# Gate and up projections of a feed-forward layer by seven half-size products

## The chip, the cores and the metric

The kernel runs on one core of a Trainium2 chip. The metric is device time in microseconds (us), the median of the runs. TensorE is called PE, its weight loads PEld, VectorE DVE, ScalarE ACT, GpSimd POOL, SyncE SP; a queue that issues DMAs has a q behind its name (SPq).

## The reference, cut to what matters

Two layers (D = 1024, hidden size 2816) work on x (512 tokens) and, beside it, on a context xc (256 tokens). Each layer has a first feed-forward half step, four mixers of 256 columns each, and a second feed-forward half step; modulation columns come from c. All is float32. The context's second half is computed in the first layer alone.

```
def swiglu(h, wg, wu, wd):
    return (jax.nn.silu(h @ wg) * (h @ wu)) @ wd
...
x = x + 0.5 * mx[2] * swiglu(pre_norm(x, norm1_g[i], mx[0], mx[1]), ffn1_wg[i], ffn1_wu[i], ffn1_wd[i])
xc = xc + 0.5 * mc[2] * swiglu(pre_norm(xc, norm1_g[i], mc[0], mc[1]), ffn1_wg[i], ffn1_wu[i], ffn1_wd[i])
...
x = x + 0.5 * mx[8] * swiglu(pre_norm(x, norm3_g[i], mx[6], mx[7]), ffn2_wg[i], ffn2_wu[i], ffn2_wd[i])
```

## The kernel before

All activations lie transposed: model columns on the partitions, tokens along the free dimension. "A" is x with 512 tokens, with halves A0 and A1 of 256, and "C" is the context with 256 (UNITS, line 28). To keep float32's accuracy on PE, each operand is split into a high and a low part of type float32r (`split`, line 262: the cast on ACT, the low part on DVE by a subtraction), and one product is three matmuls (`mm3`, line 284): high by high, high by low, low by high.

An FFN (`ffn`, line 291) runs four times: the first half step of layer 0 on A and C, the second of layer 0 on A and C, the first of layer 1 on A and C, the second of layer 1 on A alone. It has 22 blocks f of 128 hidden columns, in four groups (GROUPS, line 21: 6, 6, 5, 5). For a block, two weights of 128 x 1024 (gate and up) are loaded by SP and split (`weight`, line 273, three buffers of each kind), and PE runs 8 contraction steps of `mm3` for gate and up, on C (256 columns) and on A (512 columns): 96 matmuls. ACT takes the silu of the gate from PSUM, DVE multiplies it by up (line 323), and the result `h` is split into `hh` and `hl`. After a group, the down projection runs for the 8 output tiles m: one weight of 128 x (128 times the group's blocks), `mm3` over the blocks into `dacc`, and DVE adds the gated result into X in SBUF (line 344). In the last group the down projection goes over its weights once for C, once for A0 and once for A1 (PASSES, line 27), each time loading and splitting them again, so that the norm of a finished part (`then`) can start while the next part is computed.

Beside that run the modulation columns: `ada` (line 145) is a generator; `fill` (line 195) takes steps of it in proportion to the blocks done. A step loads 128 x 1024 weights by a DMA that POOL issues (four buffers, AB, line 23) and makes one or two reductions over 1024 elements on DVE (line 160). The first modulation columns are made at the start by PE from 32 tiles of 256 KB (`ada_first`, line 130), in the buffers of the hidden rows.

The order of instructions in each engine's queue is not that of the text: the whole program is traced, each instruction with its place in the text as its priority, and a scheduler lays out the queues at build time along a timeline that it simulates (`schedule_with_timeline_sim`, line 1569). An instruction that is ready can be drawn ahead of an earlier one that is not. Buffers of one tag are reused in turn; an instruction waits for the release of its buffer.

PSUM has eight banks in three rings (BANKS, line 29: p 4, r 2, d 2). Between the FFNs lie the output projection of the mixers (`second_half`, line 1384) and the mixers (`mixers`, line 1454) with the projections `proj` (line 427); `perm` there reads A's tokens in another order, in runs of 16.

## Time and profile before

| | us |
|---|---|
| median of 3 runs | 3223.46 |
| lowest, highest | 3222.37, 3239.32 |
| the profiled execution's own time | 3218.36 |
| its span, first to last instruction | 3216.6 |
| PE busy in it | 3092.6 |
| DVE busy in it | 1670.6 |
| ACT busy in it | 1061.2 |
| POOL busy in it | 391.3 |
[...]

The profile is of one execution. Busy time of an engine is the union of its instructions. Matmuls overlap in the pipeline, and their ends are modelled, so the step from one start to the next is the better measure of their cost. A row `A<-B,C` names the tile that is written and the tiles that are read; L270 is line 270 of the kernel.

### The profile page before, as it was taken

Reading aid. Unit: us, or ns where it says so; the run is one execution under the profiler, and the core shown is the slowest. Engines: PE = TensorE matmul, PEld = TensorE weight load, DVE = VectorE, ACT = ScalarE, POOL = GpSimd, SP = SyncE. Lnnn points to the kernel's source line nnn. Section 1 sums busy time; section 2 is a strip of 40 time slices with the busy share of each in tenths; the row PEclk is TensorE's granted clock in tenths of the full one; section 3 lists DMA queues with packets and bytes.
Section 4 is the critical chain, followed back from the end, with each engine's and each line's share of the span. In section 5 each row is a group of like instructions: output and inputs, shape, how many; then the busy total and the mean of one; then the engine's idle time right before and its main releaser. Section 6 shows DMA issues by size and latency. Waiting matters only on the chain.

```text
span 3216.6 us, 48071 instructions
## 1 busy us (share of the span) xinstructions
PE 3092.6 (96%) x19394; PEld 2699.5 (84%) x19394; DVE 1670.6 (52%) x2964; ACT 1061.2 (33%) x1912; POOL 391.3 (12%) x646
## 2 busy tenths in 40 slices
PE   7999999998999999999999999999997899999998
PEld 4888888886788888888889988888885788788887
DVE  4994232736855449994236332323646745353334
ACT  3212112545444433121224212122455353342223
POOL 1110000410233011120002000000311332000001
PEclk9999999998999999999999999999998999899999
DMA  6662221514543335683124221212523523323333
GB/s 246 200 204 59 70 68 48 176 56 125 153 98 89 85 127 180 202 264 120 53 73 125 61 64 60 73 53 68 149 74 121 149 73 83 122 87 99 96 99 105
DMA packets 133485, 358.42 MB, mean 111 GB/s; under 512 B 17968, under 2 KB 31792, under 8 KB 132880
## 3 DMA queue, kind: packets, MB, share of 16 engines
q1 hardware_dynamic: 101200, 256.52, 26.0%
q0 software_dynamic: 32064, 98.85, 10.9%
q8 instruction: 152, 2.49, 0.3%
q14 instruction: 69, 0.57, 0.1%
HBM read 317.94 MB, written 39.65 MB: 111 GB/s over the span
## 4 chain that ended last, share of the span: by engine, by line
PE 55%; DVE 3%; DMA 1%; ACT 1%; issue 1%; POOL 0%; SPq 0%; POOLq 0%; DVEq 0%; ACTq 0%
PE dacc L286 4%; PE dacc L287 4%; PE dacc L288 4%; PE uA L288 4%; PE uA L286 4%; PE uA L287 4%; PE gA L287 4%; PE gA L286 4%; PE gA L288 4%; PE guC L288 3%; PE guC L286 3%; PE guC L287 3%; PE o L738 2%; PE pj L286 1%; PE pj L288 1%; PE pj L287 1%
## 5 line engine op out<-in xcount | busy, mean ns | idle before, releaser
L265 ACT CAST wh<-wr 128x1024 fp32r<-128x1024 f32 (+5 forms) x443 | 394.8, 893 | 1262.9 <-PE dacc L287 452.8
L270 DVE TENSOR_TENSOR wl<-wr,wh 128x1024 fp32r<-128x1024 f32 (+5 forms) x443 | 459.6, 1040 | 411.3 <-ACT wh L265 391.0
L286 PE MATMUL dacc<-hh,wh 128*128 128x256 f32 (+1 forms) x1392 | 451.3, 326 | 1.7 <-ACT wh L265 1.5
L288 PE MATMUL dacc<-hh,wl 128*128 128x256 f32 (+1 forms) x1392 | 450.7, 326 | 1.4 <-DVE wl L270 1.3
L287 PE MATMUL dacc<-hl,wh 128*128 128x256 f32 (+1 forms) x1392 | 452.1, 326 | 0.0
L286 PE MATMUL guC<-xnhC,wh 128*128 128x256 f32 x1056 | 298.8, 284 | 3.3 <-ACT xnhC L259 1.7
L288 PE MATMUL guC<-xnhC,wl 128*128 128x256 f32 x1056 | 299.4, 284 | 0.9 <-DVE wl L270 0.9
L287 PE MATMUL guC<-xnlC,wh 128*128 128x256 f32 x1056 | 299.0, 283 | 0.0
L160 DVE CUSTOM_DVE_ANT_0 adao<-adaw,silr,adab 128x1024 f32<-128x1024 f32 x224 | 287.1, 1282 | 11.8 <-DMA adaw<-ada_t 8.5
L286 PE MATMUL gA<-xnhA,wh 128*128 128x512 f32 (+1 forms) x752 | 284.2, 379 | 2.0 <-ACT xnhA L259 2.0
L286 PEld LDWEIGHTS dacc<-hh,wh 128*128 128x128 f32 x1392 | 261.4, 188 | 27.7 <-ACT wh L265 2.6
L287 PE MATMUL gA<-xnlA,wh 128*128 128x512 f32 (+1 forms) x752 | 282.9, 378 | 1.0 <-DVE xnlA L260 1.0
L288 PEld LDWEIGHTS dacc<-hh,wl 128*128 128x128 f32 x1392 | 261.2, 188 | 26.9 <-DVE wl L270 2.0
L288 PE MATMUL uA<-xnhA,wl 128*128 128x512 f32 (+1 forms) x752 | 283.0, 376 | 0.6 <-DVE wl L270 0.6
L286 PE MATMUL uA<-xnhA,wh 128*128 128x512 f32 (+1 forms) x752 | 283.1, 376 | 0.4 <-ACT wh L265 0.4
L287 PE MATMUL uA<-xnlA,wh 128*128 128x512 f32 (+1 forms) x752 | 283.1, 376 | 0.0
L288 PE MATMUL gA<-xnhA,wl 128*128 128x512 f32 (+1 forms) x752 | 282.8, 376 | 0.0
L287 PEld LDWEIGHTS dacc<-hl,wh 128*128 128x128 f32 x1392 | 261.4, 188 | 25.0
L344 DVE SCALAR_TENSOR_TENSOR xA<-dacc,modG,xA 128x512 f32<-128x512 f32 (+1 forms) x160 | 102.1, 641 | 253.5 <-PE dacc L288 253.2
L286 PEld LDWEIGHTS guC<-xnhC,wh 128*128 128x128 f32 x1056 | 202.3, 192 | 7.4 <-ACT wh L265 2.4
L287 PEld LDWEIGHTS guC<-xnlC,wh 128*128 128x128 f32 x1056 | 202.9, 192 | 2.7
L288 PEld LDWEIGHTS guC<-xnhC,wl 128*128 128x128 f32 x1056 | 203.0, 192 | 1.9 <-DVE wl L270 1.5
(352 smaller groups left out, 5737.7 us busy)
## 6 DMA issues: line engine op xcount, KB each, us to landing
wr<-wgu SPq DMA_DIRECT2D x176, 512.0 KB, 3.6
adaw<-ada_t POOLq DMA_DIRECT2D x128, 512.0 KB, 4.4
wr<-wd SPq DMA_DIRECT2D x120, 320.0 KB, 3.0
wr<-wd SPq DMA_DIRECT2D x64, 384.0 KB, 3.2
wr<-win SPq DMA_DIRECT2D x44, 512.0 KB, 3.7
adaw<-ada_w SPq DMA_DIRECT2D x32, 256.0 KB, 5.2
hl<-eh SPq DMA_DIRECT2D x32, 192.0 KB, 3.1
...
```

Of the source, the lines that this page charges most:

```text
L160: nc.vector.tensor_tensor_reduce(o, w, self.silr[:, v], 1.0, self.adab[:, l, m:m + 1], ALU.mult, ALU.add, self.mods[l][:, m, v:v + 1])
L265: nc.scalar.copy(hi, src)
L270: (nc.vector if leng == "V" else nc.gpsimd).tensor_tensor(lo, src, hi.bitcast(F32), op=ALU.subtract)
L286: nc.tensor.matmul(out, lhsT=wh, rhs=xh, start=start, stop=False)
L287: nc.tensor.matmul(out, lhsT=wh, rhs=xl, start=False, stop=False)
L288: nc.tensor.matmul(out, lhsT=wl, rhs=xh, start=False, stop=stop)
L344: nc.vector.scalar_tensor_tensor(out=x, in0=acc, scalar=gate[:, i, m, r:r + 1], in1=x, op0=ALU.mult, op1=ALU.add)
L738: nc.tensor.matmul(o[:, q0 + q], lhsT=p[:, q * 128:q * 128 + 128], rhs=v(kb), start=False, stop=kb == 3 and q == n // 128 - 1)
```

## The change

The three FFNs that work on A and C get a new function, `ffn2`; the last one, on A alone, keeps `ffn` without its context parts. Blocks 0 to 2 are computed plainly, the other 19 by Strassen's scheme (in Winograd's form) with seven products in place of eight. The 2 x 2 blocks of the weight are (gate, up) by the two halves of the contraction, those of the activation are the two halves of the contraction by two halves of the tokens: 256 of A and 128 of C each, 384 columns. So xn is now laid out as two tiles of 4 contraction steps x 2 halves x 384 tokens for each part. `sums7` makes the activation's sums once per FFN, on DVE and POOL (x21 is overwritten with a sum after the plain blocks); `chunk7` makes the weight's sums for each block on DVE, splits seven blocks of 128 x 512, and runs seven products of 4 x 3 matmuls, with additions between the PSUM banks' contents on DVE. It yields after each product, and two blocks run interleaved, seven slots apart. Weights come in raw tiles of 512 columns (eight buffers) and split pairs of 512 (five buffers) instead of 1024 and three.

The groups are now six of 3 blocks and one of 4. Except in the last group, the down projection's result is scaled by ACT into a tile y (three buffers) and added to X by an accumulating DMA that POOL issues; the steps of `down` are placed between the products. In the last group all eight weights are split once and kept in the buffers of the activation's sums. A wait for the gate columns (`adone`) is met in the text by taking more steps of `ada` first. `ada` has two buffers and loads one step ahead, writes its unused result to a smaller tile, and the row `silr` is loaded after `ada_first`, which puts half of its tiles into the raw weight buffers. In the first FFN A's norm is now done in halves. `proj` with `perm` runs A in two halves.

```diff
-AB = 4
-NS, LAG = [0, 2, 2, 2], 2
+AB = 2
+LAG = 2
 NR = "r"
 SSV, SSM = ("A1",), 5
+RB, BB, WAIT = 8, 5, 3
 PASSES = {1: [["A0"], ["A1"]], 2: [["C"], ["A0"], ["A1"]]}
+GROUPS2 = [(f, f + 3) for f in range(0, 18, 3)] + [(18, 22)]
+SLOTS = 7
...
+        self.XN = {w: [p.tile([128, 4, 2, 384], F32R, name="xn%s%d" % (w, i)) for i in range(2)] for w in "hl"}
+    def xn(self, w, u, k):
+        return self.tok(self.XN[w][k // 4][:, k % 4], u)
+    def tok(self, t, u):
+        return {"A": t[:, :, 0:256], "C": t[:, :, 256:384], "A0": t[:, 0, 0:256], "A1": t[:, 1, 0:256]}[u]
+    def two(self, t, u):
+        return t.rearrange("p (h t) -> p h t", h=2) if len(u) == 1 else t
...
+        if not both:
+            self.weights(e("wp", 3, self.side_x), 1024)
+            self.fs = e("fs", 2, self.side_x)
+        else:
+            self.wp, self.wblk = e("wp", 1, self.side_x), True
+            self.raws = 0
+            self.fs = e("fs", 2, self.side_x)
         p = e("xp", 1, self.side_o)
-        self.X = {q: p.tile([128, KD, t], F32, name="x" + q) for q, t in self.T.items()}
-        self.hp = e("hp", 8, self.side_o)
+        x = p.tile([128, KD, TX + TC], F32, name="x")
+        self.X = {"A": x[:, :, 0:TX], "C": x[:, :, TX:], "": x}
+        self.hp = e("hp", 4 if both else 8, self.side_o)
+        if both:
+            self.tp7 = e("t7", 1, self.side_o)
...
+                if g >= 2:
+                    w = self.wp.tile([128, 512], F32, tag="wr", name="adaw", bufs=RB)
+                else:
+                    w = self.hp.tile([128, 768], F32, tag=("hh", "hl")[g % 2], name="adaw")[:, :512]
...
+        def load(n):
+            w = self.wa.tile([128, 1024], F32, tag="wa", name="adaw", bufs=AB)
+            if js[0][0] == 0 and js[0][1] < 8 and n < AB:
+                nc.gpsimd.tensor_copy(w[:, 0:1], self.xn("l", "A1", KD - 1)[:, 0:1].bitcast(F32))
+            nc.gpsimd.dma_start(out=w, in_=self.I["ada_t"][todo[n][0], todo[n][1]])
+            ws.append(w)
+        for n, (l, m) in enumerate(todo):
+            j = m // 8
             nv = 1 if l == 1 and j >= 5 else 2
-            for m in range(j * 8, j * 8 + 8):
-                w = self.wa.tile([128, 1024], F32, tag="wa", name="adaw", bufs=AB)
-                if l == 0 and n == 0 and m - j * 8 < AB:
-                    nc.gpsimd.tensor_copy(w[:, 0:1], self.XNl["A"][:, KD - 1, 0:1].bitcast(F32))
-                nc.gpsimd.dma_start(out=w, in_=self.I["ada_t"][l, m])
-                for v in range(nv):
-                    o = self.wa.tile([128, 1024], F32, tag="wo", name="adao", bufs=1)
-                    nc.vector.tensor_tensor_reduce(o, w, self.silr[:, v], 1.0, self.adab[:, l, m:m + 1],
-                                                   ALU.mult, ALU.add, self.mods[l][:, m, v:v + 1])
-                if m == j * 8 + 7:
-                    self.mod_cols(l, j, nv)
-                yield
+            if n == 0:
+                load(0)
+            if n + 1 < len(todo):
+                load(n + 1)
+            for v in range(nv):
+                o = self.fs.tile([128, TX], F32, tag="sq", name="adao", bufs=1).bitcast(BF16)
+                nc.vector.tensor_tensor_reduce(o, ws[n], self.silr[:, v], 1.0, self.adab[:, l, m:m + 1],
+                                               ALU.mult, ALU.add, self.mods[l][:, m, v:v + 1])
+            if m % 8 == 7:
+                self.mod_cols(l, j, nv)
+                self.adone.add((l, j))
+            yield
...
+        if self.wblk:
+            bs = [self.block(self.raw(ap[:, c:min(w, c + 512)])) for c in range(0, w, 512)]
+            return Cols([b[0] for b in bs]), Cols([b[1] for b in bs])
...
+    def raw(self, ap):
+        t = self.wp.tile([128, 512], F32, tag="wr", name="wr", bufs=RB)[:, :ap.shape[-1]]
+        self.nc.sync.dma_start(out=t, in_=ap)
+        return t
+    def block(self, src, pair=None):
+        w = src.shape[-1]
+        hi, lo = pair or [self.wp.tile([128, 512], F32R, tag="b" + t, name="w" + t, bufs=BB) for t in "hl"]
+        self.split(src, hi[:, :w], lo[:, :w])
+        return hi, lo
...
+        def down(f0, f1, m, us, last):
+            nf = f1 - f0
+            while (l, 3 * i + 2) not in self.adone:
+                self.sided += 1
+                next(self.side)
+            ap = dn[l, fi, m, :, f0:f1].rearrange("p f c -> p (f c)")
+            if not last:
+                wh, wl = self.weight(ap, nf * 128)
+            else:
+                if m not in keep:
+                    keep[m] = self.block(self.raw(ap), [keep[w][m // 3][:, m % 3] for w in "hl"])
+                wh, wl = keep[m]
+            for v in us:
+                p, cols, t = self.unit(v)
+                r = 0 if p == "A" else 1
+                acc = self.psum((128, t), name="dacc", ring=None if last else "d")
+                if not last and v == us[0]:
+                    y = self.wp.tile([128, TX + TC], F32, tag="y", name="y", bufs=3)
+                for f in range(f0, f1):
+                    c = slice((f - f0) * 128, (f - f0) * 128 + 128)
+                    self.mm3(self.two(acc, v), wh[:, c], wl[:, c], self.tok(H[f][0], v), self.tok(H[f][1], v), f == f0, f == f1 - 1)
+                if not last:
+                    nc.scalar.activation(y[:, 0:TX] if p == "A" else y[:, TX:], acc, ACTF.Copy, scale=gate[:, i, m, r:r + 1])
+                    continue
+                x = self.X[p][:, m, cols]
+                nc.vector.scalar_tensor_tensor(out=x, in0=acc, scalar=gate[:, i, m, r:r + 1], in1=x,
+                                               op0=ALU.mult, op1=ALU.add)
+                self.sumsq(v, m)
+                if p in save:
+                    nc.gpsimd.dma_start(out=self.xd[p][:, m, cols], in_=x)
+            if not last:
+                nc.gpsimd.dma_start(out=self.X[""][:, m], in_=y, accum_op=ALU.add)
+        nc1 = GROUPS2[0][1]
+        order = sorted((SLOTS * (f - nc1) + 2 * n, f, n) for f in range(nc1, NF) for n in range(SLOTS))
+        chunks, tasks, gi = {}, [(1 + m, *GROUPS2[0], m) for m in range(KD)], 1
+        for t, f, n in order:
+            if n == 0:
+                chunks[f] = self.chunk7(up[l, fi, f], hid, f)
+            next(chunks[f], None)
+            if n == SLOTS - 1 and f == GROUPS2[gi][1] - 1 and f < NF - 1:
+                tasks += [(t + WAIT, *GROUPS2[gi], m) for m in range(KD)]
+                gi += 1
+            if tasks and tasks[0][0] <= t:
+                down(*tasks.pop(0)[1:], ("C", "A"), False)
+            fill(nc1, (t + 1) / SLOTS)
+        for k in tasks:
+            down(*k[1:], ("C", "A"), False)
+        keep = {w: [self.tp7.tile([128, 3, 512], F32R, tag="t%s%d" % (w, n), name="wt" + w) for n in range(3)] for w in "hl"}
+        due = []
+        for us in PASSES[2]:
+            for m in range(KD):
+                if due and m >= LAG:
+                    then(due.pop(0))
+                down(*GROUPS2[-1], m, us, True)
+            due += us
+        for u in due:
+            then(u)
...
+        temp = lambda n: self.wp.tile([128, TX + TC], F32, tag="y", name="t7" + n, bufs=3).rearrange("p (k c) -> p k c", k=2)
+        minus = dict(scalar=-1.0, op0=ALU.mult, op1=ALU.subtract)
+        V, G = nc.vector, nc.gpsimd
+        def whole(n, pair, e):
+            x = temp(n)
+            e.tensor_tensor(x, *[p.bitcast(F32) for p in pair], op=ALU.add)
+            return x
+        xn = lambda i, j, ks: [self.XN[w][i][:, ks, j] for w in "hl"]
+        t7 = lambda n, ks: [self.T7[w][n][:, ks] for w in "hl"]
+        for ks in (slice(0, 2), slice(2, 4)):
+            x11, x12, x22 = whole("11", xn(0, 0, ks), G), whole("12", xn(0, 1, ks), V), whole("22", xn(1, 1, ks), V)
+            V.tensor_tensor(x11, x11, x12, op=ALU.subtract)
+            V.tensor_tensor(x12, x22, x12, op=ALU.subtract)
+            V.scalar_tensor_tensor(out=x22, in0=x11, in1=x22, **minus)
+            for x, n in ((x22, 1), (x11, 0), (x12, 2)):
+                self.split(x, *t7(n, ks))
+        for ks in (slice(0, 2), slice(2, 4)):
+            x21, t2 = whole("21", xn(1, 0, ks), G), whole("2", t7(1, ks), G)
+            V.scalar_tensor_tensor(out=x21, in0=t2, in1=x21, **minus)
+            self.split(x21, *xn(0, 1, ks))
...
+        A11, A21, A22, A12 = [self.raw(ap[:, j, 512 * h:512 * h + 512]) for j, h in ((0, 0), (1, 0), (1, 1), (0, 1))]
+        T = lambda n: [self.T7[w][n] for w in "hl"]
+        B = lambda i, j: [self.XN[w][i][:, :, j] for w in "hl"]
+        s = lambda: self.wp.tile([128, 512], F32, tag="ws", name="ws", bufs=4)
+        small = lambda tag: self.fs.tile([128, 384], F32, tag=tag, name=tag, bufs=1 if tag in ("u3", "sg") else 2)
+        def product(bank, src, x, first):
+            wh, wl = self.block(src)
+            for k in range(4):
+                c = slice(k * 128, k * 128 + 128)
+                self.mm3(bank, wh[:, c], wl[:, c], x[0][:, k], x[1][:, k], first and k == 0, k == 3, True)
+        add = lambda e, o, a, b, op=ALU.add: e.tensor_tensor(o, a, b, op=op)
+        a = self.psum((128, 384), name="pa", ring="p")
+        product(a, A11, B(0, 0), True)
+        s1 = small("s1")
+        nc.scalar.copy(s1, a)
+        yield
+        b = self.psum((128, 384), name="pb", ring="p")
+        S1, S2 = s(), s()
+        add(nc.vector, S1, A21, A22)
+        add(nc.vector, S2, S1, A11)
+        product(b, S2, T(1), True)
+        u2 = small("u2")
+        add(nc.vector, u2, b, s1)
+        yield
+        c = self.psum((128, 384), name="pc", ring="r")
+        product(c, S1, T(0), True)
+        S3, S4 = s(), s()
+        add(nc.vector, S3, A11, A21)
+        add(nc.vector, S4, A12, S2)
+        yield
+        product(b, S3, T(2), False)
+        u3 = small("u3")
+        add(nc.vector, u3, b, s1)
+        add(nc.vector, u3, c, u3)
+        yield
+        product(a, A12, B(1, 0), False)
+        sg = small("sg")
+        nc.scalar.activation(sg, a, ACTF.Silu)
+        yield
+        product(c, S4, B(1, 1), False)
+        add(nc.vector, u2, c, u2)
+        nc.scalar.activation(u2, u2, ACTF.Silu)
+        hh, hl = hid(f)
+        nc.vector.scalar_tensor_tensor(out=u3, in0=u2, scalar=-1.0, in1=u3, op0=ALU.mult, op1=ALU.mult)
+        self.split(u3, hh[:, 1], hl[:, 1])
+        yield
+        product(b, A22, B(0, 1), False)
+        add(nc.vector, s1, b, s1)
+        nc.vector.scalar_tensor_tensor(out=s1, in0=sg, scalar=-1.0, in1=s1, op0=ALU.mult, op1=ALU.mult)
+        self.split(s1, hh[:, 0], hl[:, 0])
...
+            for u in self.units([p], halves or (perm and p == "A")):
                 c = self.unit(u)[1]
-                o, v = ps[:M, c], lambda a: a[:, c]
                 if perm and p == "A":
-                    o = o.rearrange("p (b r c) -> p b r c", b=4, r=8)
-                    v = lambda a: a.rearrange("p (r b c) -> p b r c", b=4, r=8)
+                    h = int(u[1])
+                    o = ps[:M].rearrange("p (b r c) -> p b r c", b=4, r=8)[:, :, 4 * h:4 * h + 4]
+                    v = lambda a: a.rearrange("p (r b c) -> p b r c", b=4, r=4)
+                else:
+                    o, v = self.two(ps[:M, c], u), lambda a: a
                 for k in range(KD):
                     self.mm3(o, wh[:, k * 128:k * 128 + M], wl[:, k * 128:k * 128 + M],
-                             v(self.XNh[p][:, k]), v(self.XNl[p][:, k]), k == 0, k == KD - 1)
+                             v(self.xn("h", u, k)), v(self.xn("l", u, k)), k == 0, k == KD - 1)
```

## Rows read from the trace of the kernel before

**Rows 1.** part 1 of the page: busy us, share of the span, instructions

```profile
PE 3092.6 (96%) x19394; PEld 2699.5 (84%) x19394; DVE 1670.6 (52%) x2964; ACT 1061.2 (33%) x1912; POOL 391.3 (12%) x646
```

**Rows 2.** busy time by stage: PE, PEld, DVE, ACT, POOL; clock; DMA share; GB/s

```profile
320.00:400.00 80.00, 80.00 (x462) 70.44 (x461) 24.21 (x32) 15.40 (x22) 0.00 (x0) 1.00 0.23 69
80.00:160.00 80.00, 80.00 (x462) 70.72 (x461) 75.13 (x122) 18.05 (x28) 11.82 (x22) 1.00 0.65 201
```

**Rows 3.** single tiles, two stages: ns min/median/max, first and last start us

```profile
L286 PE MATMUL guC<-xnhC,wh x80: 277/283/283, 351.0 to 423.1; 128*128 128x256 f32 x80
...
L286 PE MATMUL gA<-xnhA,wh x40: 389/389/396, 356.8 to 428.2; 128*128 128x512 f32 x40
...
L288 PE MATMUL uA<-xnhA,wl x40: 389/389/389, 362.7 to 434.1; 128*128 128x512 f32 x40
...
L286 PE MATMUL dacc<-hh,wh x96: 277/336/397, 300.7 to 350.3; 128*128 128x256 f32 x48, 128*128 128x512 f32 x48
```

**Rows 4.** DVE by line and shape: count, busy us, mean ns, idle before

```profile
L270 DVE TENSOR_TENSOR wl<-wr,wh 128x768 fp32r<-128x768 f32 x72 | 68.5, 954 | 30.9 <-ACT wh L265 25.8 <-PE wo L288 5.1
...
L270 DVE TENSOR_TENSOR hl<-h,hh 128x512 fp32r<-128x512 f32 x88 | 60.4, 686 | 0.0
...
L344 DVE SCALAR_TENSOR_TENSOR xA<-dacc,modG,xA 128x256 f32<-128x256 f32 x64 | 30.1, 476 | 6.1 <-PE dacc L288 6.0
...
L270 DVE TENSOR_TENSOR hl<-h,hh 128x256 fp32r<-128x256 f32 x66 | 28.0, 424 | 20.8 <-ACT hh L265 20.8
...
L323 DVE TENSOR_TENSOR h<-sg,guC 128x256 f32<-128x256 f32 x66 | 27.8, 421 | 162.6 <-ACT sg L322 162.6
```

**Rows 5.** tile adaw: ns min/median/max; 65 to 160 us (PE, PEld, DVE, POOL); landing

```profile
L160 DVE CUSTOM_DVE_ANT_0 adao<-adaw,silr,adab x224: 1274/1281/1287, 67.3 to 1464.3; 128x1024 f32<-128x1024 f32 x112
...
65.00:160.00 95.00, 0.00 (x0) 0.00 (x0) 61.54 (x48) 13.34 (x25) 1.00 0.66 208
...
DMA to landing us min/median/max: 3.7/4.7/12.0
```

**Rows 6.** ACT groups by line and shape, as rows 4

```profile
L265 ACT CAST hh<-h 128x512 fp32r<-128x512 f32 x88 | 54.7, 622 | 9.4 <-DVE h L323 7.3
...
L322 ACT ACTIVATE sg<-gA 128x512 f32<-128x512 f32 x88 | 51.7, 587 | 0.0
...
L265 ACT CAST hh<-h 128x256 fp32r<-128x256 f32 x66 | 26.8, 407 | 34.2 <-DVE h L323 31.8 <-DMA adaw<-ada_t 2.3
```

**Rows 7.** DVE in order of time, one plain block: start us, us, instruction

```profile
363.35 1.23 DVE L270 TENSOR_TENSOR wl<-wr,wh 128x1024 fp32r<-128x1024 f32 x1 [4.63 <-ACT wh L265]
367.96 0.69 DVE L323 TENSOR_TENSOR h<-sg,uA 128x512 f32<-128x512 f32 x1 [3.38 <-PE uA L288]
368.79 1.23 DVE L270 TENSOR_TENSOR wl<-wr,wh 128x1024 fp32r<-128x1024 f32 x1
```

**Rows 8.** single tiles: ns min/median/max, first and last start

```profile
L270 DVE TENSOR_TENSOR wl<-wr,wh x443: 281/1217/1775, 31.5 to 3203.0; 128x1024 fp32r<-128x1024 f32 x78, 128x640 fp32r<-128x640 f32 x39, 128x768 fp32r<-128x768 f32 x24, 128x384 fp32r<-128x384 f32 x3
...
L222 POOL TENSOR_TENSOR ssA<-ssA,sq x48: 726/832/1401, 581.1 to 3203.7; 128x256 f32<-128x256 f32 x48
```

**Rows 9.** DMA issues: KB each, us to landing; then landings of xdA (POOL)

```profile
wr<-wd SPq DMA_DIRECT2D x120, 320.0 KB, 3.0
...
qa<-hl POOLq DMA_DIRECT2D x8, 384.0 KB, 6.9
...
DMA to landing us min/median/max: 2.1/3.4/6.8
```

**Rows 10.** the start in order of time

```profile
23.48 1.60 SPq L278 DMA_DIRECT2D wr<-wgu  x3
...
46.40 0.51 PE L286 MATMUL guC<-xnhC,wh 128*128 128x256 f32 x2 [1.55 <-ACT xnhC L259]
```

**Rows 11.** PE in a permuted projection, in order of time

```profile
865.54 0.41 PE L288 MATMUL pj<-xnhA,wl 128*128 128x512 f32 x1
865.79 0.41 PE L286 MATMUL pj<-xnhA,wh 128*128 128x512 f32 x1
```

222 lines of the change are left out of this document (140 added, 82 removed).

## The prediction

> **What bounds the kernel now.** I read the page's first part, then stages, then single lines. TensorE (PE) is busy for 96% of the span, VectorE (DVE) for 52% [rows 1]. In two 80 us stages inside the first feed-forward block (FFN) PE is busy for all 80 us at a granted clock of 1.00, whether DVE is at 24.21 or at 75.13 us, and PE issues the same 462 matmuls [rows 2]. So in the FFNs the column count on PE sets the time, and neither a loaded DVE nor DMA slows a matmul. DMA's share in those stages is 0.23 and 0.65 [rows 2].
>
> What does a matmul cost? Rows 3 give starts, not modelled ends. Five plain blocks run from 351.0 to 434.1 + 0.2 us: 16.67 us each. In one, C's 48 matmuls of 256 columns take 356.8 - 351.0 = 5.8 us, 0.121 us each; A's 48 of 512 columns take the other 10.87 us, 0.226 each. The down stage of six blocks and eight outputs takes 351.0 - 300.7 = 50.3 us, 1.05 us for a block and output [rows 3].
>
> **Part 1: seven products.** A plain block has 96 matmuls (48 of 512, 48 of 256 columns). The new one has 7 x 4 x 3 = 84 of 384 columns. The trace has no such product; 384 lies halfway between 256 and 512, so (0.121 + 0.226)/2 = 0.1736 us, 14.58 us a block. That saves 2.09 us; 19 blocks in each of three FFNs: 57 x 2.09 = **119.0 us**, all on PE, the path that sets the end. Down keeps its columns, as do the first three blocks.
>
> **What DVE must do for it.** Per block: 4 weight sums and 7 low halves of 512 at 0.686 us (7.55), 7 two-source operations of 384 (five on PSUM, two low halves) at 0.555, halfway between 0.424 and 0.686 (3.89), and 2 scalar-tensor-tensor at 0.476 + 0.131 = 0.607 (1.21) [rows 4]: 12.65 us, 1.81 per product against 12 x 0.1736 = 2.08 us of PE. Three blocks with their eight downs are 3 x 14.58 + 8 x 3.14 = 68.9 us of PE and 3 x 12.65 + 8 x 0.555 = 42.4 us of DVE. The first FFN adds 96 modulation reductions of 1.281 us [rows 5], 123 us over its some 520, 16 per 68.9 us: 58.6 in all. ACT: 7 casts of 0.622, three PSUM reads of some 0.49 and 2 casts of 0.515 per block, some 1.49 per down: 32.4 of 68.9 us [rows 6]. Both fit, so PE stays the bound on average. The cover for each split (0.622 + 0.686 = 1.3 us) is the five block buffers: four products, 8.3 us, ahead.
>
> **Stalls at the edges.** In the first FFN DVE has, before the first derived product: 24 norm steps of two operations at some 0.48 (23.0), 12 low halves (8.2), 9 pairs of activation operations at 2 x 0.424 (7.6), 16 reductions for the gate columns (20.5), 16 sums and splits of 768 at 0.954 (15.3): 74.6 us from some 42 us on, so to 117 us. PE has 50.0 us of plain blocks and one product, until 94 us, and then eight downs of 3.14 us as filler if the gate columns are there. Between 0 and 22 us; I take 6, nearer to the filled end, since work is drawn ahead now too [rows 7]. In each FFN the last block's products have no partner, and its last one is followed by about 2.2 us of DVE and ACT with 1 us of matmuls to cover it; with the entry, 3 us each. Together **+15** (0 to +45).
>
> [...]
>
> **Updates by accumulating DMA.** 144 evictions move from DVE to ACT, a scratch tile and a POOL-issued DMA. POOL pays some 0.56 us per issue; behind a waiting update stand the next modulation loads, POOL's sums and its square sums. No accumulating DMA is in the trace; the nearest POOL transfers land in 2.1 to 6.9 us, at most 12.0 [rows 5, 9]. A scratch tile is held for 2.1 + 0.6 + 0.56 + landing, at most 15.3 us; there are three and one is wanted per product and down, 2.08 + 3.14 = 5.22 us, so up to 15.7 us nothing waits. Cost 0 (0 to +5). SP gets about 4 weight issues for 2 in each block, of smaller size (320 KB land in 3.0 us [rows 9]): hidden by eight raw buffers, 0. The two (not four) modulation buffers: (4.7 + 2.56 + 0.5)/2 = 3.9 us for a unit, as now (95/24 [rows 5]); 0 to +5.
>
> **Start.** At 23.48 us SP issues three 512 KB weights before the second half of the first modulation weights; first matmul at 46.40 [rows 10]. Now 1 MB of weights and the 1 MB broadcast row come after. Part of that is needed anyway; the sixteen 256 KB tiles took some 17 us, so 0.5 to 1.5 MB are 2 to 6 us. Against it: weights now wait for buffers that these tiles use. **-4** (-8 to +3).
>
> **Projections and layout.** 12 permuted projections become halves: 288 x (2 x 0.121 - 0.226) = 4.4 us at most; they already step at 0.24 [rows 11], so 0 to 4.4, I take **+2**. A's 512 columns are now two runs. Runs of 16 cost 0.24 against 0.226; on some 2000 matmuls that would be 27 us, but one break is nearer to none than to 31: 0. Pools released in another order at four transitions: 0, -5 to +5.
>
> **Sum**, against the profiled execution (3218.4 us, span 3216.6; the median of the runs is 5 us higher): 3218.4 - 119.0 + 15 - 4 + 2 = **3112**. Its own range: all low ends 3086, all high ends (without the layout) 3167.
>
> **Rivals.**
> *DVE binds where the reductions run.* Now 96 reductions take 123 us of DVE in 190 us (two stretches like [rows 5]). If they keep that rate beside the products, DVE needs 190 x 42.4/68.9 = 117 + 123 = 240 us in 190: +50, so 3162. For: reductions run as soon as a load lands. Against: they stand later in the program than the splits of their block, so splits win when both are ready.
>
> *The matmul of 384 columns is dearer.* The gain is gone at 16.67/84 = 0.198 us. With the strided surcharge (0.014) it is 0.187: +65, so 3177. Against: 0.121 and 0.226 differ by the columns, and the rate holds from stage to stage [rows 2, 3].
>
> *Slower: DVE's order puts PSUM reads ahead of the next split.* In the text each product is followed by the addition that reads its bank, and the next product's split comes after. If DVE keeps that order, PE waits for an addition (0.555) and a low half (0.686) after 4 of 7 products: 4 x 1.2 x 57 = 274 us, so 3386; it turns slower from 119/228 = 0.5 us per event on. Against: the present order isn't the text's. At 363.35 and 368.79 DVE splits the next block's weights before and between the steps of the current block's hidden row (367.96) [rows 7], and PE stays busy throughout [rows 2]. [...] In half measure (0.5 us per event) the gain just goes: no change.
>
> *Slower: the accumulating DMA lands late.* From 16 us on, a scratch tile is missing, ACT stops, and splits with it. At 20 us landing: (23.3/3 - 5.22) x 144 = 366, so 3480.
>
> **How the numbers follow.** Forecast 0.58; DVE binds 0.15; dearer matmul 0.04; order in half measure 0.07; order in full 0.11; late updates 0.05. A measurement here tells 0.5%, 16 us, from no change. Faster: 0.58 + 0.15 + 0.04 = 0.77; same 0.07; slower 0.16. The range from 3086 to 3205 leaves out the last two and part of the half measure, some 0.2.
>
> **What would show it.** Right: seven-product stretches with PE busy at 1.00 and starts 0.174 us apart, blocks of 14.6 us in place of 16.7, FFNs of some 520 us in place of 560, DVE near 60 to 85% there. DVE rival: wl ends PE's waits between 50 and 250 us only. Order rival: PE idle before each product with DVE as releaser, in all three FFNs, and a granted clock below 1.00. Update rival: ACT's y waits on a DMA, landings of over 16 us. The forecast is wrong if the time saved on products is there but the FFNs do not shrink by 40 us.

## The result and the profile after

The changed kernel is slower: 3247.12 us against 3223.97, a ratio of 1.0073 with a 95% interval of 1.0058 to 1.0088. The forecast was 3112. The profiled execution spans 3244.9 us (before: 3216.6), 28.3 more. Where they come in is read from the first and last matmul of each stretch:

| stretch, from matmul to matmul | before, us | after, us | difference |
|---|---|---|---|
| start to the first FFN's first matmul | 46.4 | 55.4 | +9.0 |
| first FFN | 559.7 | 539.9 | -19.8 |
| behind it, to the first projection | 4.1 | 26.8 | +22.7 |
| mixers of layer 0 and output projection | 588.5 | 592.5 | +4.0 |
| to the second FFN | 0.2 | 12.6 | +12.4 |
| second and third FFN | 1121.1 | 1098.0 | -23.1 |
| behind them | 4.7 | 18.3 | +13.6 |
| mixers of layer 1 | 505.6 | 513.3 | +7.7 |
| rest | 386.3 | 388.1 | +1.8 |

The FFNs shrink by 42.9 us, not by 119, and the transitions give 48.7 back. Part 1 of the page, to be held against [rows 1]: PE has 66 us less to do in a longer span, DVE 357 us more.

```profile
PE 3026.7 (93%) x18880; PEld 2730.5 (84%) x18880; DVE 2027.8 (62%) x3766; ACT 1362.1 (42%) x2655; POOL 560.6 (17%) x814
```

The products themselves cost what was forecast. PE in order of time (start us, us, instruction) shows one product of twelve matmuls, from 544.06 to the next one's 546.16: 2.10 us with the hand-over, 0.174 for each step inside.

```profile
544.06 0.33 PE L370 MATMUL pb<-th,wh 128*128 128x384 f32 x1
544.23 0.34 PE L371 MATMUL pb<-tl,wh 128*128 128x384 f32 x1
...
546.16 0.34 PE L370 MATMUL pc<-xnh,wh 128*128 128x384 f32 x1
```

Where PE then loses time, the stages show (PE, PEld, DVE, ACT, POOL busy; granted clock, DMA share, GB/s):

```profile
112.00:200.00 88.00, 77.55 (x414) 70.81 (x413) 81.79 (x142) 35.93 (x69) 17.70 (x26) 0.96 0.68 186
400.00:440.00 40.00, 40.00 (x233) 38.70 (x232) 24.73 (x45) 17.81 (x34) 3.19 (x4) 1.00 0.40 92
600.00:640.00 40.00, 21.75 (x133) 19.42 (x133) 29.69 (x68) 22.99 (x49) 10.38 (x21) 0.64 0.24 73
1280.00:1320.00 40.00, 32.54 (x160) 28.73 (x159) 39.05 (x59) 15.66 (x32) 12.37 (x10) 0.87 0.34 99
1840.00:1880.00 40.00, 33.27 (x168) 30.20 (x167) 34.39 (x51) 16.06 (x32) 15.41 (x15) 0.87 0.57 163
```

From 400 us on the seven products run without a gap. At the head of each seven-product stretch PE is idle for 7 to 10 us in 40 to 88, with DVE busy for 86 to 98% of the time; in the stage behind the first FFN it is idle for nearly half. A stretch is the time from an FFN's first product to its last; what lies before it, from the FFN's first matmul on, is called its plain part. At the median step of each form of matmul, without waits, a stretch would take some 431 us; the three take 449.6, 452.7 and 448.9.

### The profile page after: what moved, and what is told of

Read it like the earlier page. It is cut to its first block, busy times and chain, and to the rows that moved or that the text cites. A ratio compares the mean times of both kernels' runs of the same rounds, so it can differ in the third digit from the quotient of the medians.

```text
span 3244.9 us, 49733 instructions
## 1 busy us (share of the span) xinstructions
PE 3026.7 (93%) x18880; PEld 2730.5 (84%) x18880; DVE 2027.8 (62%) x3766; ACT 1362.1 (42%) x2655; POOL 560.6 (17%) x814
## 3 DMA queue, kind: packets, MB, share of 16 engines
q0 software_dynamic: 52800, 155.48, 20.6%
## 4 chain that ended last, share of the span: by engine, by line
PE 76%; DVE 10%; DMA 5%; issue 5%; ACT 2%; POOL 1%; SPq 0%; DVEq 0%; POOLq 0%; ACTq 0%
PE dacc L370 6%; PE dacc L372 6%; PE dacc L371 6%; PE pb L370 3%; PE pb L371 3%; PE pb L372 3%; PE o L1012 3%; PE pj L370 3%; PE pj L372 3%; PE pj L371 3%; PE pc L370 2%; PE pa L372 2%; PE pc L372 2%; PE pc L371 2%; PE pa L370 2%
## 5 line engine op out<-in xcount | busy, mean ns | idle before, releaser
L334 ACT CAST wh<-wr 128x512 fp32r<-128x512 f32 (+6 forms) x523 | 348.6, 669 | 657.1 <-PE dacc L371 150.1
L339 DVE TENSOR_TENSOR wl<-wr,wh 128x512 fp32r<-128x512 f32 (+6 forms) x523 | 393.1, 754 | 266.4 <-ACT wh L334 254.0
L371 PE MATMUL dacc<-hl,wh 128*128 128x512 f32 (+1 forms) x1080 | 369.0, 342 | 9.6 <-DVE hl L339 9.6
L370 PE MATMUL dacc<-hh,wh 128*128 128x512 f32 (+1 forms) x1080 | 368.5, 343 | 1.9 <-ACT hh L334 0.9
L372 PE MATMUL dacc<-hh,wl 128*128 128x512 f32 (+1 forms) x1080 | 367.7, 342 | 1.4 <-DVE wl L339 1.4
L211 DVE CUSTOM_DVE_ANT_0 adao<-adaw,silr,adab 128x1024 bf16<-128x1024 f32 x224 | 293.2, 1309 | 35.2 <-DMA adaw<-ada_t 34.8
L370 PE MATMUL pj<-xnh,wh 128*128 128x256 f32 (+2 forms) x768 | 249.8, 326 | 5.5 <-ACT wh L334 5.0
L372 PE MATMUL pj<-xnh,wl 128*128 128x256 f32 (+2 forms) x768 | 244.0, 321 | 9.1 <-DVE wl L339 9.0
L371 PE MATMUL pj<-xnl,wh 128*128 128x256 f32 (+2 forms) x768 | 246.2, 321 | 0.0
L500 ACT ACTIVATE y<-dacc,modG 128x256 f32<-128x256 f32 (+1 forms) x288 | 166.1, 579 | 67.6 <-PE dacc L372 26.7
```

The lines of the kernel that those rows point to most:

```text
L211: nc.vector.tensor_tensor_reduce(o, ws[n], self.silr[:, v], 1.0, self.adab[:, l, m:m + 1], ALU.mult, ALU.add, self.mods[l][:, m, v:v + 1])
L334: nc.scalar.copy(hi, src)
L339: (nc.vector if leng == "V" else nc.gpsimd).tensor_tensor(lo, src, hi.bitcast(F32), op=ALU.subtract)
L370: nc.tensor.matmul(out, lhsT=wh, rhs=xh, start=start, stop=False, skip_group_check=more)
L371: nc.tensor.matmul(out, lhsT=wh, rhs=xl, start=False, stop=False, skip_group_check=more)
L372: nc.tensor.matmul(out, lhsT=wl, rhs=xh, start=False, stop=stop, skip_group_check=more)
```

## Experiments

Each run is the changed kernel with the edit named; the ratio is to the kernel before, run beside it (the changed kernel: 1.0073). What a run gained is the difference of the medians; the intervals reach 4 to 11 us to either side. Every edit makes the scheduler lay out all queues anew, so things can move that the edit does not name; places are therefore given beside the times.

| run | us | ratio, 95% interval |
|---|---|---|
| e1 two square tiles | 3245.1 | 1.0061 (1.0046 to 1.0076) |
| e2 reductions cut | 3250.2 | 1.0070 (1.0046 to 1.0093) |
| e3 products' sums on DVE | 3227.3 | 1.0011 (0.9989 to 1.0032) |
| e4 rings back | 3239.7 | 1.0045 (1.0029 to 1.0062) |
| e5 reductions and loads cut | 3209.8 | 0.9946 (0.9913 to 0.9979) |
| e6 norms' sums on DVE | 3228.8 | 1.0013 (1.0001 to 1.0025) |
| e7 modulation loads on SP | 3239.1 | 1.0063 (1.0041 to 1.0085) |
| e8 e3, e4, e6 and a bank | 3213.5 | 0.9967 (0.9950 to 0.9983) |
| e9 modulation paced | 3222.1 | 0.9985 (0.9968 to 1.0002) |
| e10 e8 and e9 | 3198.7 | 0.9905 (0.9880 to 0.9931) |
| e11 e10, gate moved | 3169.2 | 0.9821 (0.9796 to 0.9846) |
| e12 e11, later updates | 3164.3 | 0.9821 (0.9799 to 0.9844) |
| e13 e11, first gate's reductions cut | 3150.6 | 0.9773 (0.9750 to 0.9797) |
| e14 third norm's bank | 3250.3 | 1.0091 (1.0059 to 1.0124) |

### The norms behind the FFNs (e1, e6)

The changed kernel behind its first FFN, PE in order of time (in brackets: idle before, and what ended it). Three norms, C, A0 and A1, follow one another after the last down matmul, and the first projection stands behind the last:

```profile
595.27 0.28 PE L372 MATMUL dacc<-hh,wtl 128*128 128x256 f32 x1
599.00 1.01 PE L294 MATMUL nsum<-ones,ssC 128*128 128x1 f32 x4 [3.45 <-POOL ssC L283]
...
608.70 1.01 PE L294 MATMUL nsum<-ones,ssA 128*128 128x1 f32 x4 [5.44 <-POOL ssA L283]
...
618.35 1.01 PE L294 MATMUL nsum<-ones,ssA 128*128 128x1 f32 x4 [5.00 <-DVE ssA L283]
621.46 1.19 PE L301 MATMUL rb<-dg,ones 128*128 128x256 f32 x2 [2.10 <-DVE dg L297]
622.09 0.78 PE L370 MATMUL pj<-xnh,wh 128*96 128x256 f32 x1
```

C's rows of x were final from 573 us on. Theory A blamed the square, which has one tile where it had two:

```diff
-            sq = self.fs.tile([128, TX], F32, tag="sq", name="sq", bufs=1 if self.wblk else 2)[:, :t]
+            sq = self.fs.tile([128, 384], F32, tag=("sg", "u3")[m % 2], name="sq", bufs=1)[:, :t]
```

> The changed kernel with one edit: the squares of the norms alternate between two tiles that are idle at the time, as they did between two buffers in the kernel before, instead of sharing one. Theory A (one square tile makes the square on ScalarE and its sum on GpSimd take turns, and the norm behind each FFN comes late): the three stretches without matmuls behind the FFNs, 26.8, 12.6 and 18.3 us in the changed kernel, fall toward the 4.1, 0.2 and 4.7 of the kernel before, together by 25 to 50 us, and the time goes to 3195 to 3222. Rival B (these norms are late because GpSimd's queue and VectorE are full, not for the lack of a tile): the three stretches shrink by less than 10 us together, time 3237 to 3247.

The three gaps were 23.0, 20.6 and 13.0 us, 56.6 together against 57.7: theory A falls. POOL's queue in the changed kernel, in order of time, shows what else delays the sum:

```profile
586.98 0.75 POOL L283 TENSOR_TENSOR ssC<-ssC,sq 128x256 f32<-128x256 f32 x1
587.73 0.57 POOL L507 DMA_DIRECT2D xdA<-x  x1
589.18 0.54 POOL L507 DMA_DIRECT2D xdA<-x  x1 [0.88 <-DVE x L503]
...
592.05 0.54 POOL L507 DMA_DIRECT2D xdA<-x  x1 [0.90 <-DVE x L503]
592.61 0.75 POOL L283 TENSOR_TENSOR ssC<-ssC,sq 128x256 f32<-128x256 f32 x1
```

Between two adds for C stand four stores of A's rows, and each waits for DVE's next row, 1.44 us apart. C's adds are laid out one in 5.6 us, behind work of a later pass.

```diff
-            (eng or (nc.vector if u == "A" or (u in SSV and m >= SSM) else nc.gpsimd)).tensor_tensor(ss, ss, sq, op=ALU.add)
+            (eng or (nc.vector if self.wblk or u == "A" or (u in SSV and m >= SSM) else nc.gpsimd)).tensor_tensor(ss, ss, sq, op=ALU.add)
```

> The changed kernel with the adds of the norms' squares on VectorE instead of GpSimd. Theory A2 (those adds stand in GpSimd's queue between stores that each wait for the next row of x, one add in about 6 us, so that the norms of C and of the first half of A come only after the last matmul; the two-tile run left that order as it was): with GpSimd out of the chain the row sum of C comes while the halves of A are multiplied, the three stretches without matmuls fall from 26.8, 12.6 and 18.3 us to 8 to 14, 2 to 8 and 8 to 14, and as TensorE's granted clock falls less behind them (0.64 to 0.79 in those 40 us now), the time falls by 30 to 55 us. Rival (the last row sums, of the second half of A, set the gap whatever the engine): the gaps shrink by 3 to 5 us each, the time by 10 to 15.

PE of this run in the same place:

```profile
584.45 0.50 PE L294 MATMUL nsum<-ones,ssC 128*128 128x1 f32 x4
...
593.69 0.50 PE L294 MATMUL nsum<-ones,ssA 128*128 128x1 f32 x4
...
603.05 1.01 PE L294 MATMUL nsum<-ones,ssA 128*128 128x1 f32 x4 [2.82 <-DVE ssA L283]
...
608.00 0.53 PE L370 MATMUL pj<-xnh,wh 128*96 128x256 f32 x1 [0.58 <-ACT wh L334]
```

The first two norms now run among down matmuls, and the gaps are 8.2, 12.3 and 8.4 us: 28.8 of the 57.7 are gone. The time fell by 18 us, less than A2's 30: the first seven-product stretch grew to 454.0, and the gap of 12.3 before the second FFN hardly moved. A2 holds for the gaps behind the first and the third FFN, where it was read.

### The stream of modulations (e2, e5, e7, e9)

```diff
-                nc.vector.tensor_tensor_reduce(o, ws[n], self.silr[:, v], 1.0, self.adab[:, l, m:m + 1],
+                nc.vector.tensor_tensor_reduce(o[:, :64], ws[n][:, :64], self.silr[:, v, :64], 1.0, self.adab[:, l, m:m + 1],
```

> The changed kernel with the reductions of the modulation cut to 64 of their 1024 columns (most of each modulation sum is left out; loads, waits and order are the same). Theory B (VectorE is the bound at the start of each FFN, because the reductions of 1.28 us are drawn in between norm steps, splits and sums there): the plain blocks go from 57 to 64 us each to about 50, the seven-product stretches from 449 to about 430, and 60 to 90 us of the time go: 3157 to 3187. Rival (the order in which VectorE reads PSUM in the seven-product blocks holds TensorE, reductions or not): the seven-product stretches stay at 445 to 450 each, and the time falls by less than 25 us.

Nothing was gained (3250.2): the stretches took 463.7, 447.9 and 446.9 us. By the numbers this favours the rival, but the stage shows another cause:

```profile
112.00:200.00 88.00, 74.92 (x402) 67.16 (x400) 49.40 (x171) 32.20 (x64) 21.35 (x34) 0.98 0.84 239
```

DVE is busy for 49.40 us in place of 81.79, but PE still loses 13 us. What DVE waited for in this stage of e2 (us, times, longest) says why:

```profile
DVE adao L211 <- DMA adaw<-ada_t: 38.0, 22, 3.5
```

Nearly all of DVE's 38.6 idle us lie in front of a cut reduction whose load has not landed. No wait of PE, ACT or DVE in the stage ends with a weight load of the FFN, so the weights did not come late, as the expectation of e5 has it. The reductions kept their places in DVE's queue among the splits; tiles that are reduced at once are refilled at once (the DMA share goes from 0.68 to 0.84), and the work that was cut came back as waiting in the same queue. e5 cuts the loads as well:

```diff
-            nc.gpsimd.dma_start(out=w, in_=self.I["ada_t"][todo[n][0], todo[n][1]])
+            nc.gpsimd.dma_start(out=w[:, :64], in_=self.I["ada_t"][todo[n][0], todo[n][1]][:, :64])
```

> The changed kernel with both the loads and the reductions of the modulation cut to 64 of 1024 columns (most of each modulation sum and of its traffic is left out), where the run before had cut only the reductions and its weights came late instead: there the DMA share rose from 0.67 to 0.89 in the 40 us from 120, and the first seven-product stretch took 463.7 us. Theory B2 (the stream of modulation weights is the load at the start of each FFN, as VectorE time when its tiles are reduced at the old pace and as traffic in front of the weights when they are reduced faster): the seven-product stretches go from 449 to 428 to 435 each, the waits of TensorE for wl there nearly vanish, and the time falls by 45 to 75 us. Rival (the traffic of weights and updates alone, or the order of VectorE's queue, holds the first blocks): the stretches stay at 442 or more, the time falls by less than 25.

The time fell by 37 us; the stretches took 447.7, 440.9 and 437.7, between theory and rival, and the second FFN's plain part 58.0 in place of 63.8. The stream is a cause of the loss, and e5 does not take all of it away. In the first stretch, only 2 us shorter, DVE waited in front of cut reductions for 27.4 us of the 88, 18 times. One such wait from both sides, DVE and then PE of e5:

```profile
147.83 0.28 DVE L211 CUSTOM_DVE_ANT_0 adao<-adaw,silr,adab 128x64 bf16<-128x64 f32 x1 [3.12 <-DMA adaw<-ada_t]
148.04 0.08 DVE L211 DVE_READ_ACCUMULATOR2_ANT mod<- 128x1 f32 x1
148.04 0.69 DVE L339 TENSOR_TENSOR wl<-ws,wh 128x512 fp32r<-128x512 f32 x1
```

```profile
148.79 0.69 PE L372 MATMUL pc<-xnh,wl 128*128 128x384 f32 x1 [3.11 <-DVE wl L339]
```

The low half that PE lacks stands behind the reduction in DVE's queue.

What a stretch takes with no reduction beside it, e1 shows by chance. Its edit is not about the stream, but in its queues 32 reductions run in the last 80 us before the second FFN, 96 in that FFN's plain part and stretch and none in the third FFN (changed kernel: 4, 76 and 48). Its second stretch took 460.7 us (452.7), its third 430.4 (448.9): that is the time without waits, with all of the products' sums still in the FFN. The first 40 us of that stretch, to be held against the stage from 1840 us above:

```profile
1863.00:1903.00 40.00, 40.00 (x233) 37.39 (x232) 19.05 (x34) 18.54 (x37) 4.34 (x5) 1.00 0.52 114
```

e1 as a whole gained 2 us, since the second FFN grew and the mixers of layer 0 took 610.1 us in place of 592.5.

Can the stream be kept and its place be changed? e7 moved the loads to SP's queue:

```diff
-            nc.gpsimd.dma_start(out=w, in_=self.I["ada_t"][todo[n][0], todo[n][1]])
+            nc.sync.dma_start(out=w, in_=self.I["ada_t"][todo[n][0], todo[n][1]])
```

> The changed kernel with the loads of the modulation's weights issued by SyncE, in the queue of the FFN's weight loads, instead of GpSimd. Theory B2 (these loads and their reductions run ahead of need at the start of each FFN): in a queue with the weights they can run no further ahead than the eight weight buffers, the reductions spread over the FFN, the seven-product stretches go from 449 toward 435, and the time falls by 20 to 45 us. Rival (a load that waits for one of its two buffers now holds the weight loads behind it): TensorE waits for wh and wl more than before, the stretches grow to 455 or more, the time rises by 10 to 40.

The reductions began in each 40 us as early as ever (17, 14, 16, 12, 16, 12 from 120 us; changed kernel: 17, 14, 14, 14, 15, 12), and the intervals of the two ratios overlap: it says nothing of spreading. e9 gives each load something to wait for:

```diff
+            if len(self.done) > 1:
+                nc.gpsimd.tensor_copy(w[:, 0:1], self.done[-2][:, 0, 0:1].bitcast(F32))
             nc.gpsimd.dma_start(out=w, in_=self.I["ada_t"][todo[n][0], todo[n][1]])
```

(`done` holds the low parts of the hidden rows, in the order of the blocks.)

> The changed kernel with each load of modulation weights held, by a one-column copy on GpSimd in front of it, until the hidden rows of the block before the last are done; nothing else changes. In the run that issued them from SyncE the reductions came as early as ever (17, 14, 16, 12 of them in each 40 us from 120), so that run said nothing of spreading them. Theory B2 (VectorE and the traffic of the reductions at the start hold the first seven-product blocks; without the stream the time fell by 35 us): spread to the last quarter of the FFN, the stretches go from 449 to 440 to 445 and the time falls by 10 to 25 us. Rival (what the stream costs is its amount, wherever it lies, or the copies hold GpSimd's queue with the updates behind them): time within 6 us of the changed kernel, or later.

Now the last reduction of the first FFN starts at 498.6 us (365.6 before) and the time falls by 25 us. By place: the second FFN's plain part takes 55.1 (63.8), the third's stretch 436.5 (448.9); the first stretch stays at 449.0, the second at 452.9. The mechanism holds, in two places of four.

### Sums on two engines (e3)

DVE and then POOL of the changed kernel, at the head of the second FFN's stretch:

```profile
1291.35 0.95 DVE L339 TENSOR_TENSOR tl<-t,th 128x768 fp32r<-128x768 f32 x1
1292.22 2.34 DVE L339 TENSOR_TENSOR wl<-ws,wh 128x512 fp32r<-128x512 f32 x1
1294.48 2.86 DVE L211 CUSTOM_DVE_ANT_0 adao<-adaw,silr,adab 128x1024 bf16<-128x1024 f32 x1
...
1299.88 2.30 DVE L339 TENSOR_TENSOR wl<-ws,wh 128x512 fp32r<-128x512 f32 x1
```

```profile
1291.58 2.43 POOL L549 TENSOR_TENSOR t<-xnh,xnl 128x768 f32<-128x768 f32 x1 [1.46 <-DVE t L558]
1293.98 2.29 POOL L549 TENSOR_TENSOR t<-th,tl 128x768 f32<-128x768 f32 x1
1299.44 2.20 POOL L549 TENSOR_TENSOR t<-xnh,xnl 128x768 f32<-128x768 f32 x1 [3.18 <-DVE tl L339]
```

```diff
-        V, G = nc.vector, nc.gpsimd
+        V = G = nc.vector
```

> The changed kernel with all sums of weights and inputs of the seven products on VectorE, none on GpSimd. Theory C (GpSimd's sums of 2.2 to 2.8 us and VectorE's operations beside them slow each other: a low part of 0.69 us took 2.34 beside one): the slow operations are gone and the seven-product stretches of 449 us shrink by 3 to 10 us each, the time by 5 to 30 us. Rival (VectorE's busy time is the bound there, and the sums only add to it, about half of the sums times 0.7 us): the stretches grow by 2 to 10 us each, time 3250 to 3277.

Theory C holds: 20 us, with more work on DVE. The stretches took 445.0, 440.4 and 447.1. Tile ws, low halves of 512, ns minimum, median and maximum, in the changed kernel and then in e3:

```profile
L339 DVE TENSOR_TENSOR wl<-ws,wh x228: 671/691/2344, 111.0 to 2278.9; 128x512 fp32r<-128x512 f32 x114
```

```profile
L339 DVE TENSOR_TENSOR wl<-ws,wh x228: 671/690/696, 103.5 to 2259.9; 128x512 fp32r<-128x512 f32 x114
```

The low half, which reads two tiles (ws and wh), took 2.34 us beside a POOL sum in the changed kernel, and at most 0.696 us in e3, without one.

### The start (e4, e14, e8)

PE in the changed kernel, in order of time:

```profile
42.57 0.50 PE L294 MATMUL nsum<-ones,ssC 128*128 128x1 f32 x4
...
53.88 1.01 PE L294 MATMUL nsum<-ones,ssA 128*128 128x1 f32 x4 [2.76 <-DVE nt L324]
55.40 0.58 PE L370 MATMUL gu<-xnh,wh 128*128 128x256 f32 x1 [0.51 <-ACT xnh L328]
```

C's row sum waits at 42.57 for a bank of the ring that `ada_first` now shares with the norms, and A1's waits at 53.88 for the bank that C's norm still reads, ahead of the first gate matmul.

```diff
-        acc = self.psum(name="adaacc", ring="r")
+        acc = self.psum(name="adaacc")
...
-        tp = self.psum((128, 4, 128), name="adatp", ring="r")
+        tp = self.psum((128, 4, 128), name="adatp")
```

> The changed kernel with the two PSUM tiles of the modulation's chain back in the rings that they had in the kernel before, instead of the two-bank ring of the norms. Theory D (the first norm's row sum waits for a bank that the modulation's tiles hold, so the first FFN starts 9 us later): the first matmul of the first FFN comes at 45 to 48 us instead of 55.4, and the time falls by 6 to 10 us, to 3237 to 3241. Rival (the later start is due to the first inputs' arrival on a fuller queue): the first matmul stays at 54 to 56 and the time within 3 us.

C's row sum came at 24.6 us, the first gate matmul at 54.6: theory D falls. A1's sum waited all the same, to 52.64, but in both kernels the row of the first gate matmul names a cast (xnh) as the last thing that it waited for. It is A0's first (from 54.84 to 55.35 us in the changed kernel), whose norm steps stand in DVE's queue behind all eight of C's. The time fell by 7 us, as forecast but not by the forecast cause, in no one place, and the intervals of the two ratios overlap.

```diff
-        rb = self.rstd_bc(self.sums(u), t // 128, D, NR)
+        rb = self.rstd_bc(self.sums(u), t // 128, D, "d" if self.wblk and u == "A1" else NR)
```

> The changed kernel with one edit: row sum and broadcast of the norm of A's second half in the PSUM ring of the last accumulators instead of the norms' two banks. Theory D2 (three norms share two banks now; the third's row sum stands in TensorE's queue ahead of the first gate matmul and waits until the last step of C's norm has read its bank, 53.88 us): the first matmul of the first FFN comes at 47 to 50 us instead of 55.4, and the time falls by 4 to 9 us. Rival (what comes first on TensorE is late anyway, as giving the modulation its rings back moved it by 0.8 us only): the first matmul stays at 54 or later, the time within 3 us.

Alone it gains nothing either: the first gate matmul, now one of C's, comes at 56.2 us, behind A1's broadcast at 53.86. e8 has both edits, with those of e3 and e6:

> The changed kernel with four edits together: the norms' adds on VectorE, the sums of the seven products on VectorE, the modulation's PSUM tiles in their old rings, and the row sum and broadcast of the second half of A in another PSUM ring (today the third norm waits for the bank of the first, and TensorE's first gate matmul stands behind it in the queue). If the effects add (20 and 8 us as the single runs measured, 30 to 55 as expected of the norms, 5 to 8 for the bank): 60 to 90 us below the changed kernel, 3157 to 3187, faster than the kernel before. If VectorE is full, the two moves onto it take from each other: 3195 to 3215.

The first gate matmul, C's again, starts at 52.1 us. DVE and PE of e8, then of e14:

```profile
51.07 0.86 DVE L324 SCALAR_TENSOR_TENSOR nt<-x,modA,rb 128x256 f32<-128x256 f32 x2
52.09 0.55 PE L370 MATMUL gu<-xnh,wh 128*128 128x256 f32 x1 [9.33 <-ACT xnh L328]
```

```profile
55.54 0.48 DVE L324 SCALAR_TENSOR_TENSOR nt<-x,modA,rb 128x256 f32<-128x256 f32 x1
56.17 0.55 PE L370 MATMUL gu<-xnh,wh 128*128 128x256 f32 x1 [1.09 <-DVE nt L324]
```

In both runs this DVE row ends with the eighth and last step of C's norm, and PE starts some 0.15 us after it (51.93 and 56.02 us), though C's first cast started at 45.10 us in e8. In `ffn2` the tile for C's gate and up takes a bank of ring r (`ring="r" if u == "C"`), the norms' two banks; in the kernel before, `guC` came from the other rings. So it gets its bank when C's norm has read it for the last time, where PE before began at 46.40, after C's first cast [rows 10]. That is argued from these rows and the kernel's text; a run with C's tile in another ring wasn't made.

In time e8 is 34 us below the changed kernel, which is the second case. The single runs e3, e6, e4 and e14 gave 20, 18, 7 and -3 us, 42 together, so that the edits take from each other is not clear of the noise in the time. It is seen by place: DVE is busy for 40.00 of the 40 us from 80, from 1200 and from 1240, the second FFN's plain part grew from 63.8 to 69.7 us and the first stretch from 449.6 to 455.3 (the others: 441.8 and 446.5).

### What is left in the first stretch, and a better kernel (e10 to e13)

> The run with four edits together (sums of norms and of products on VectorE, rings, bank) with the same pacing of the modulation. If VectorE's fullness at the start is what was left there (it was busy 40 of 40 us from 80 and from 1200, and the first stretch took 455.3 us): the three stretches go from 455, 442 and 446 to 435 to 442, and the time to 3185 to 3203. Rival (the forced first eight units and the splits alone fill VectorE there): within 6 us of 3213.5.

3198.7 us; stretches of 459.1, 455.0 and 437.7. The forecast time came, but not from the forecast places, so by luck: the first two stretches grew, the third shrank, and the plain part of the second FFN fell from 69.7 to 51.9.

```diff
-                    self.beside([(0, j) for j in range(2, 8)])
+                    self.beside([(0, j) for j in range(2, 9)])
...
-                    self.beside([(0, 8)] + [(1, j) for j in range(4)])
+                    self.beside([(1, j) for j in range(4)])
```

> The same, and in addition the eight units that the second FFN must have before its first update (its own gate) are done in the stream of the first FFN, with its 48. If VectorE's load at the start of the second FFN delays its plain blocks (69.7 us in the run of four edits, VectorE busy 80 of 80 us from 1200): the plain part falls to 54 to 60 us and the time by another 6 to 15 us. Rival (its norms and splits alone hold it): plain part still 65 or more, time within 4 us of the run beside it.

The plain part was short already and stays (52.4); the second stretch falls from 455.0 to 438.4, as the 16 reductions that its first update needs are no longer in it. The medians differ by 29.5 us, the profiled executions by 12.3, and only these can be placed; e10's was its fastest by 15 us. In the first stretch, still 456.3, PE's waits (us, times, longest) and DVE show the same need:

```profile
PE dacc L373 <- ACT y L505: 5.2, 1, 5.2
```

```profile
134.20 1.28 DVE L213 CUSTOM_DVE_ANT_0 adao<-adaw,silr,adab 128x1024 bf16<-128x1024 f32 x1
135.40 0.08 DVE L213 DVE_READ_ACCUMULATOR2_ANT mod<- 128x1 f32 x1
135.51 0.17 DVE L243 TENSOR_SCALAR modG<-mod 128x16 f32<-128x16 f32 x1
```

Two runs ask whether the early update or its reductions are the cost:

```diff
-        chunks, tasks, gi = {}, [(1 + m, *GROUPS2[0], m) for m in range(KD)], 1
+        chunks, tasks, gi = {}, [(7 + m, *GROUPS2[0], m) for m in range(KD)], 1
```

> The run with the gate moved, and the updates of the plain group emitted from the seventh piece of the seven-product stretch on instead of the first. Theory G (the first updates come before their gate and their last hidden rows are there: in the run with the gate moved, TensorE waited 5.2 us at 130.7 to 136.3 for a bank whose copy needs the gate, ready at 135.5, and in the changed kernel 4.1 and 4.0 us for hl in the later FFNs): the first stretch goes from 456.3 to 449 or less, the time falls by 5 to 12 us. Rival (VectorE's backlog holds whatever product is there, updates or not): the stretches stay within 3 us, the time too.

The stretch stays at 455.3, the ratio at 0.9821: theory G falls. PE's wait of 5.2 us for y is gone, and one of 5.1 us for a low half (wl) has come in its place.

```diff
+                cw = 64 if js[0] == (0, 2) and n < 8 else 1024
-                nc.vector.tensor_tensor_reduce(o, ws[n], self.silr[:, v], 1.0, self.adab[:, l, m:m + 1],
+                nc.vector.tensor_tensor_reduce(o[:, :cw], ws[n][:, :cw], self.silr[:, v, :cw], 1.0, self.adab[:, l, m:m + 1],
```

> The run with the gate moved, and in it the 16 reductions of the first FFN's own gate cut to 64 of 1024 columns (that gate is then wrong by what is left out; loads and order stay). Starting the updates later had left the first stretch at 455.3 us. Theory H (those 16 reductions of 1.28 us, which the first update must have, stand in VectorE's queue among the first splits and sums): the first stretch falls from 456.3 to 436 to 445, its gate is ready some 15 us before 135.5, the time falls by 8 to 18 us. Rival (the splits and sums of the first blocks alone keep VectorE full): the stretch stays above 450, the time within 5 us.

The gate is ready at 119.9 us, the stretch takes 439.9, and the stage from 112 us has 9 us more of PE than e11's 76.53:

```profile
112.00:200.00 88.00, 85.80 (x479) 80.92 (x478) 77.41 (x146) 37.31 (x71) 23.74 (x41) 0.98 0.73 202
```

Theory H holds: 16 reductions, 20 us of DVE in front of the first update, were 16 of the 25 us that the first stretch of e11 took beyond the 431; 9 us are left. e11 and e12 leave nothing out and are faster than both kernels, by 1.8% against the kernel before.

## Why the prediction was wrong, point by point

| term | forecast, us | measured, us |
|---|---|---|
| seven products | -119.0 | -118 |
| edges inside the FFNs | +15 | +75 |
| start | -4 | +9.0 |
| projections | +2 | +2.1 |
| the rest of the mixers, and behind them | none | +9.6 and +1.8 |
| transitions | 0 | +48.7 |

(-42.9 for the FFNs is -118 + 75, rounded. Against the median step of each form of matmul, PE's excess in the three FFNs was 16 us before and 91 after: steps of over four times the median 58 in place of 8, shorter ones 33 in place of 8. What is left of the difference is put down to the products.)

- **Part 1, right.** The step between 0.121 and 0.226 was 0.174 us, blocks took 14.6, and the cover of a split holds in steady state (PE busy for 40.00 of 40 us at 400). The rival of a dearer matmul falls. So does that of DVE's order as it was stated: PE's losses lie at the heads of the stretches, not before each product. What stands wrongly in DVE's order are reductions, not PSUM reads (e2, e5). The layout term, 0, was right too: a projection's step with A's 512 columns in two runs was 0.227 us, as before.
- **The step that failed: stalls at the edges.** It counted DVE's backlog for the first FFN alone; the 3 us for each FFN stand for its entry and last block, and for the later FFNs it has no backlog. They have one: the second has a norm, sums and the reductions of its own gate in the same 80 us. It also took "work is drawn ahead now too" as a help; here the reductions were drawn ahead of splits, though their place is spread over the FFN. The rival in which DVE binds where reductions run (chance 0.15, +50 us) had most of the mechanism, but in its "against" the splits win when both are ready. e5 puts 37 us down to the stream, and e1's third stretch, with no reduction beside it, loses nothing. e2 adds what no rival had: a shortened reduction still held the splits behind it while its load was on the way, in the stage from 112 us for 38.0 us of DVE in 22 waits.
- **Sums on POOL beside DVE, for which the sum has no term, were worth 20 us (e3).** In the changed kernel a low half of 512 took up to 2.344 us beside a POOL sum, in e3 at most 0.696. Here too the later FFNs count most: 14.4 of the 20.6 us between the two profiled executions lie in them.
- **Transitions at 0, the second step that failed.** "Pools released in another order" was costed; the norms' adds in POOL's queue, between stores that wait for DVE, weren't. What stands in a queue behind a waiting instruction was asked for the updates alone. e6 takes half of the gaps away with one engine's name.
- **Start.** Loads were weighed; banks weren't. The ring of the norms' two banks got the modulation's tiles, a third norm and C's gate and up as further users, and 9 us were lost where -4 stood. That C's norm has to end before C's first matmul is read from e8 and e14; no run took it away.
- **Projections, right.** 576 halves at 0.118 us in place of 288 matmuls at 0.24 took 73.7 us in place of 71.6.
- **Updates, right.** Accumulating transfers of 384 KB land in 5.0 us in the median and 9.6 at most. With the 3.3 us that the prediction adds for the rest of the hold that is 12.9, below the 15.7 from which a scratch tile would be missing (its update rival takes 16 us for the landing alone; by its own sum 12.4 would be enough). Only POOL's issue is dearer, 871 ns in place of the 560 of the stores in the kernel before:

```profile
L509 POOL DMA_DIRECT2D x<-y x144 | 125.4, 871 | 741.3 <-ACT y L500 721.2 <-ACT wh L334 10.9 <-PE pb L372 5.9
...
x<-y POOLq DMA_DIRECT2D x144, 384.0 KB, 5.0
```

- **Open.** Of the mixers' other 9.6 us some 5 lie in layer 0's output projection (76.0 us in place of 71.1); what causes these and the rest isn't known, and in e12 the mixers of layer 1 still take 518.0 us against 505.6. Gaps of 6.6 to 9.0 us behind the FFNs remain in e12 as well, and why the queues were laid out with C's adds behind A's stores isn't known.
